# A hybrid decoder block: the gate's sigmoid from exp and log beside the attention, the transposes a step later, the residual added by an accumulating DMA

## The chip, the cores and the metric

The kernel runs on one core of a Trainium2 chip. The metric is the device time of one execution in microseconds; before the change it is 2204.19 us, the median of three runs (2201.32 to 2206.55). One execution was taken by the hardware profiler; it took 2203.55 us, and 2201.8 us of it lie between its first and its last instruction (the span). Profile lines name the engines: PE is the matrix engine (matmuls; PEld its weight loads), DVE the vector engine, ACT the scalar engine that evaluates exp, log and the like, POOL the GpSimd engine, SP the engine that only issues DMAs. Every engine executes its own list of instructions in order; an instruction that waits holds up all that stand behind it on its engine.

## The reference

One layer on 528 positions (16 learned ones ahead of 512 real ones) of width 2048, all in float32:

```python
hn = rmsnorm(h, norm_mix_g)
proj = hn @ w_in                                  # u (1024 wide), q, k, v (16 heads of 64)
y_ssm = s5_mixer(u)                               # diagonal state-space scan, GELU, then the gate:
#       y = y * sigmoid(y @ w_glu + b_glu)
y_attn = stick_breaking_attention(q, k, v)
#       z = q k^T / 8;  keep = log_sigmoid(-z) on valid keys
#       w = exp(log_sigmoid(z) + sum of keep over the later keys);  y = w v
h = h + concat(rmsnorm(y_ssm, g_ssm), rmsnorm(y_attn, g_attn)) @ w_out
hn = rmsnorm(h, norm_ffn_g)
gate, val = split(causal_depthwise_conv(hn @ w_up, 3 taps))
h = h + (silu(gate) * val) @ w_down               # 5632 wide
out = rmsnorm(h, norm_final_g)[16:]
```

## The kernel before

Everything stands transposed: channels lie on the 128 partitions, positions along the free axis. A matmul in full float32 precision is made of three fast ones (`mm3`, lines 319 to 321): each operand is split into a high part and the rest, and high times high, high times rest and rest times high are added in one PSUM bank. So each weight tile (128 by 1024) is loaded by SP, cast to its high part on ACT (`wh`, line 241), and the rest is made on DVE (`wl`, line 117 called from line 259). These splits are written two weight tiles ahead of their use.

The stages follow each other on PE: the input projection (`u` first, then k, v and q for four units of four heads each), the gate of the state-space branch (`w_glu`, eight weight tiles j, lines 1268 to 1286), the output projection in two passes (first the half that reads the state-space branch, 16 output tiles, line 1301; then the half that reads the attention, line 1385), the feed-forward up projection with a scheme of seven products, and the down projection. Between the passes and the up projection stand two places where the helper lanes are run out (`drain`).

Beside these dense stages a second stream of work runs, written as Python generators ("lanes"). While the dense matmuls are written out, `pulse` adds the nanoseconds of each group of three to a credit, and each time the credit reaches a period it takes one step of the lane. So the order of the lane's instructions among the dense ones, on every engine, is fixed when the program is written. The attention lane takes a step per `PERATT` = 900 ns of dense work. An attention unit is a preparation (k and q split, v transposed) and twelve items (a block of queries with some heads), two steps for each. An item goes through four parts that are set some steps apart by `LAGS` = (2, 4, 6):

- `stage_a`: the scores on PE, the copy out of PSUM and Abs, Exp, Ln on ACT (`at`, lines 981 to 984);
- `stage_a2`, two steps later, on DVE: max and add, a scan along the keys against a tile of ones (`steady`), and a subtraction (lines 991 to 997);
- `stage_b`, four steps after `stage_a`: PE transposes the result (line 1018; line 1008 for the last item) and ACT takes exp;
- `stage_c`, six steps after: the product with v on PE (line 1057) and the copy out on DVE (line 1064).

During the gate, and in the last input-projection tile ahead of it, `hold[0]` is set and `pulse` does nothing: the attention lane stands still. Per gate tile j there are two halves of 24 matmuls of 260 columns; after each, ACT takes the sigmoid from PSUM with the bias, and DVE multiplies with y (line 111, tile 128 x 2 x 130). After the second half ACT scales by the norm gain (line 1282), DVE makes the rest (line 1283), ACT squares, POOL adds up the squares. Sigmoid is in another function table of ACT than exp and log, so a table is loaded ahead of the gate and another behind it.

The output projection's first pass takes each output tile from PSUM with a DVE multiplication (line 1308). Then `ssm_done` loads the residual `x` through SP and POOL adds it (line 1296). `h` is used again in the second pass.

At the start nine matmuls on the tile of ones warm PE while the first inputs are on their way (line 1167).

Of the kernel before, what the change touches and what calls it, by code (L numbers as in the profile page):

```python
# [15 lines left out]
AF = mybir.ActivationFunctionType  # L16
ALU = mybir.AluOpType
# [3 lines left out]
P = 128  # L21
# [4 lines left out]
T0 = 14  # L26
LT = L - T0
# [4 lines left out]
NC4 = L // 4  # L32
NEG = -1.0e30
PERIOD = 1600.0
PERATT = 900.0

SLACK = 3
PERX = 1100.0
HOLD = True

MIR = 60
LAGS = (2, 4, 6)

V_GMIX, V_GSSM, V_GATT, V_GFFN, V_GFIN, V_BGLU, V_CB = 0, 16, 24, 32, 48, 64, 72
V_CW = V_CB + 2 * NF
# [15 lines left out]
def build(tc, io, nslots=67, manual=True):  # L61
    nc = tc.nc
    ctx = ExitStack()
    with ctx:
# [11 lines left out]
        def open_phase(name):  # L76
            if phase[0] is not None:
                phase[1].__exit__(None, None, None)
            phase[0] = None
            if name:  # L80
                phase[1] = tc.tile_pool(name=name, bufs=2)
                phase[0] = phase[1].__enter__()

        def small(shape, tag, dt=F32, bufs=1):
            uid[0] += 1
            return phase[0].tile(list(shape), dt, tag=tag, bufs=bufs, name=f"{tag}_{uid[0]}")

        V, S, G, PE = nc.vector, nc.scalar, nc.gpsimd, nc.tensor
        uid = [0]

        def slot(shape, dt=F32):
            uid[0] += 1
            return sl.tile(list(shape), dt, tag="s", name=f"s{uid[0]}")
# [3 lines left out]
        def act(out, in_, func, **kw):  # L97

            if func in (AF.Exp, AF.Ln):
                if table[0] != "explog":  # L100
                    S.preload_act_table_set("natural_log_exp_and_others")
                table[0] = "explog"
            elif func not in (AF.Abs, AF.Square, AF.Copy, AF.Identity):
                table[0] = func
            S.activation(out, in_, func, **kw)  # L105
# [4 lines left out]
        def mul(e, out, a, b):  # L110
            e.tensor_tensor(out, a, b, op=ALU.mult)  # L111

        def add(e, out, a, b):
            e.tensor_tensor(out, a, b, op=ALU.add)  # L114
# [6 lines left out]
        def vcol(off, j):  # L121
            return vec[:, off + j : off + j + 1]
# [8 lines left out]
        steady = cst.tile([P, L], F32, name="steady")  # L131
# [160 lines left out]
        lanes = []  # L292
        credit = [0.0]
        period = [PERIOD]
        hold = [False]

        def step():
            for g in list(lanes[0]):
                if next(g, "end") == "end":
                    lanes[0].remove(g)  # L300
            if not lanes[0]:
                lanes.pop(0)

        def pulse(ns):

            if hold[0]:
                return
            credit[0] += ns
            while credit[0] >= period[0]:
                credit[0] -= period[0]  # L310
                if lanes:
                    step()
# [10 lines left out]
        def bank(shape, pool=psd, tag="d"):  # L323
            uid[0] += 1
            return pool.tile(list(shape), F32, tag=tag, name=f"{tag}{uid[0]}")
# [10 lines left out]
        def dense(kts, halves, evac, mid=None, cut=lambda x, a, b: x[:, a:b]):  # L336

            n = len(kts)
            widths = [int(np.prod(cut(kts[0][0], a, b).shape[1:])) for a, b in halves]
            pss = [dbank([P, x]) for x in widths]  # L340
            for k in range(0, n, 8):
                w = next_w()
                for i, (a, b) in enumerate(halves):
                    for j in range(8):
                        xh, xl = kts[k + j]
                        mm3(pss[i], w[0][:, j, :], w[1][:, j, :], cut(xh, a, b), cut(xl, a, b), k + j == 0, k + j == n - 1)
                        if j < 7:
                            pulse(1.4 * widths[i])
                    if i == 0:
                        ahead()  # L350
                    if mid:
                        mid(k, i)
                    if k + 8 >= n:
                        evac(pss[i], a, b)
# [34 lines left out]
        def acc_square(acc, first, x, n):  # L389
            if first:  # L390
                act(acc[:, :n], x, AF.Square)
            else:
                q = slot([P, 528])
                act(q[:, :n], x, AF.Square)
                add(G, acc[:, :n], acc[:, :n], q[:, :n])
# [461 lines left out]
        QT, KTS, VT = 0, 1, 2  # L857
# [2 lines left out]
        ydone = dram.tile([8, P, LT], F32, name="ydone")  # L860

        def at_tile(n, m):
            return small([P, 528], "at", bufs=6)[:n, :m]

        class Unit:

# [60 lines left out]
            def stage_a(self, it):  # L927
# [18 lines left out]
                else:  # L946
# [32 lines left out]
                    if j == 0:  # L979
                        self.kf = self.qf = None  # L980
                t = at_tile(n, m)
                act(t, z, AF.Abs)
                act(t, t, AF.Exp, scale=-1.0)
# [95 lines left out]
        def att_lane():  # L1079
            open_phase("att")  # L1080
            period[0] = PERATT
            todo = {}
            now = [0]
            A2, B, C = LAGS

# [68 lines left out]
                add(V, accx[:, :L], accx[:, :L], q[:, :L])  # L1154
            xraw[k] = None

        G.memset(steady, 1.0)
        G.memset(epsc, EPS)

        nc.scalar.dma_start(vec, io["vec"])  # L1160
# [2 lines left out]
        act(cst.tile([P, 1], F32, name="warm"), epsc, AF.Square)  # L1163

        ps = bank([P, 264])
        for i in range(9):
            PE.matmul(ps, steady[:, :P], steady[:, :264], start=True, stop=True)
        load_x(1)
        load_x(2)
# [18 lines left out]
        for k in range(KT):  # L1188
            for j in range(3):
                i = 3 * k + j  # L1190
# [54 lines left out]
        for un in range(4):  # L1245
            for what, base in ((KTS, 16), (VT, 24), (QT, 8)):
                for p in range(2):
                    t = slot([P, L])

                    def evac(ps, a, b):  # L1250
                        if what == QT:
                            V.scalar_tensor_tensor(t[:, a:b], ps, 0.125, rstd[:, a:b], op0=ALU.mult, op1=ALU.mult)
                        else:
                            mul(V, t[:, a:b], ps, rstd[:, a:b])

                    hf = HQ if what == QT else HF
                    hold[0] = (un, what, p) == (3, QT, 1)
                    dense(xg, hf, evac, ready_y if (un, what, p) == (3, QT, 1) else None)
                    nc.sync.dma_start(qkv[what, 2 * un + p, :, hf[0][0] :], t[:, hf[0][0] :])
            qkv_ready[0] = un + 1  # L1260
# [3 lines left out]
        HG = [(0, 2), (2, 4)]  # L1264
        accs = slot([P, 528])
        y2 = []
        hold[0] = True
        for j in range(8):
            sg = slot([P, 4, NC4 - 2])
            yy = slot([P, L])  # L1270
            yr = yraw[j]
            yraw[j] = None
            y2.append((slot([P, LT], F32R), slot([P, LT], F32R)))

            def gate(ps, a, b):
                act(sg[:, a:b, :], ps.rearrange("p (t c) -> p t c", t=2), AF.Sigmoid, bias=vcol(V_BGLU, j))
                mul(V, yy[:, 8:].rearrange("p (c t) -> p t c", t=4)[:, a:b, :], yr[:, a:b, 2:], sg[:, a:b, :])

            dense(ys, HG, gate, cut=lambda x, a, b: x[:, a:b, 2:])
            for a, b in [(T0, L)] if j < 7 else [(T0, 272), (272, L)]:  # L1280
                r = slice(a - T0, b - T0)
                S.mul(y2[j][0][:, r], yy[:, a:b], vcol(V_GSSM, j))
                V.scalar_tensor_tensor(
                    y2[j][1][:, r], yy[:, a:b], vcol(V_GSSM, j), y2[j][0][:, r].bitcast(F32), op0=ALU.mult, op1=ALU.subtract
                )
            acc_square(accs, j == 0, yy[:, T0:], LT)
        hold[0] = False
        ys = yraw = None


        h = []

        def ssm_done(o, t):
            x = slot([P, LT])
            nc.sync.dma_start(x, io["xT"][o][:, T0:])
            add(G, t, t, x)
            h.append(t)


# [1 line left out]
        for o in range(KT):  # L1301
            t = slot([P, LT])

            def evac(ps, a, b):
                if o < 2:
                    S.copy(t[:, a:b], ps)
                else:
                    mul(V, t[:, a:b], ps, rs[:, a:b])

            dense(y2, HT, evac, (lambda k, i: rms(rs, accs, HT[i : i + 1], 1024, (psd, "d"))) if o == 1 else None)  # L1310
            if o == 0:
                t0 = t
            if o == 1:
                for x in (t0, t):
                    mul(V, x, x, rs[:, :LT])
                ssm_done(0, t0)
            if o:
                ssm_done(o, t)
# [66 lines left out]
        for o in ORD:  # L1385
            dense(ya, HT, lambda ps, a, b: add(V, h[o][:, a:b], h[o][:, a:b], ps))
            x = h[o]
# [140 lines left out]
        for c in range(ND):  # L1528
            for o in range(KT):
                w = next_w()  # L1530
                ps = bank([P, SEQ])
# [15 lines left out]
        for o2 in range(8):  # L1547
            w = next_w()
            for oo in range(2):
                o = 2 * o2 + oo  # L1550
                ps = bank([P, SEQ])
# [35 lines left out]
        for a, b in ((0, 256), (256, 512)):  # L1587
            for o in range(KT):
                w = ws[o // 2]
                ps = bank([P, 256])  # L1590
# [109 lines left out]
```

## Time and profile before

| what | value |
|---|---|
| median of three runs | 2204.19 us (2201.32 to 2206.55) |
| the profiled execution, its span | 2203.55 us, 2201.8 us |
| PE busy | 2155.4 us (98%) |
| DVE busy | 1570.7 us (71%) |
| ACT busy | 1052.7 us (48%) |
| POOL busy | 209.7 us (10%) |
| attention units 0 and 1, beside the k, v, q projections | about 366 to 487 us |
| the gate, attention held | 494 to 541 us |
| units 2 and 3, beside the first pass of the output projection | 541 to 672 us |
| end of the attention lane, second pass | 672 to 772 us |
| up and down projections | from 772 us to the end |

A busy PE is not a PE at its peak: matmuls are pipelined and overlap in the records, so waits shorter than about 0.15 us do not show as idle time. What is read from the profile is where PE sits idle, what it waited for, and how the other engines' instructions follow each other there.

### The profile page before, as it was taken

What the parts mean: (1) busy time and instruction counts of PE and PEld (TensorE: products, weight loads), DVE (VectorE), ACT (ScalarE), POOL (GpSimd) and SP (SyncE); (2) the same over time, 40 slices, a digit from 0 to 9 for tenths busy, and PEclk for the clock granted to TensorE, in tenths of its full rate; (3) what the DMA queues carried; (4) which work ended last, traced back from release to release, by engine and by line L of the source; (5) the groups of instructions that cost most, each with busy time, mean ns of one, the idle gap of its engine ahead of it and who ended that gap; (6) DMA issues with size and microseconds to landing.
All of it is one profiled execution on the core that took longest, in us unless ns stands there. A gap on an engine that the chain in (4) does not pass through costs nothing.

```text
span 2201.8 us, 39840 instructions
## 1 busy us (share of the span) xinstructions
PE 2155.4 (98%) x16222; PEld 2042.1 (93%) x16222; DVE 1570.7 (71%) x2363; ACT 1052.7 (48%) x1692; POOL 209.7 (10%) x290
## 2 busy tenths in 40 slices
PE   9999999999899999999999999999999999999997
PEld 9999999889789989999999999999999888888887
DVE  7977885775876778887887788778778544444454
ACT  6255444775773555455555554554555222222235
POOL 0000000001112321111111111111110000000004
PEclk9999999999999999999999999999999999999999
DMA  6433324342333367777777777777777433333342
GB/s 221 120 109 111 114 91 135 103 127 92 116 108 102 128 167 197 197 193 194 194 207 187 194 198 194 196 193 205 187 193 222 160 122 117 120 118 117 115 144 77
DMA packets 118806, 335.10 MB, mean 152 GB/s; under 512 B 13024, under 2 KB 25696, under 8 KB 118624
## 3 DMA queue, kind: packets, MB, share of 16 engines
q1 hardware_dynamic: 100144, 269.34, 38.2%
q0 software_dynamic: 17472, 61.89, 13.7%
q8 instruction: 127, 2.08, 0.4%
q10 hardware_dynamic: 1008, 1.33, 0.2%
q14 instruction: 55, 0.45, 0.1%
HBM read 300.23 MB, written 32.28 MB: 151 GB/s over the span
## 4 chain that ended last, share of the span: by engine, by line
PE 63%; DVE 2%; issue 1%; ACT 1%; DVEq 0%; ACTq 0%
PE d L320 15%; PE d L319 15%; PE d L321 15%; PE z L320 4%; PE z L319 4%; PE z L321 4%; PE y L320 2%; PE y L319 2%; PE y L321 2%; DVE s L117 0%; DVE wl L117 0%; ACT wh L241 0%; ACT s L1356 0%; DVE s L114 0%; DVE s L111 0%
## 5 line engine op out<-in xcount | busy, mean ns | idle before, releaser
L319 PE MATMUL d<-s,wh 128*128 128x258 f32 (+4 forms) x3456 | 1061.8, 307 | 6.4 <-DVE s L111 2.7
L320 PE MATMUL d<-s,wh 128*128 128x258 f32 (+4 forms) x3456 | 1054.8, 305 | 2.2 <-DVE s L117 1.2
L321 PE MATMUL d<-s,wl 128*128 128x258 f32 (+4 forms) x3456 | 1051.3, 304 | 1.2 <-DVE wl L117 1.2
L319 PEld LDWEIGHTS d<-s,wh 128*128 128x128 f32 x3456 | 653.8, 189 | 37.8 <-DVE s L114 2.7
L320 PEld LDWEIGHTS d<-s,wh 128*128 128x128 f32 x3456 | 656.6, 190 | 31.6 <-DVE s L117 2.5
L321 PEld LDWEIGHTS d<-s,wl 128*128 128x128 f32 x3456 | 658.2, 190 | 29.9 <-DVE wl L117 1.8
L241 ACT CAST wh<-wr 128x1024 fp32r<-128x1024 f32 (+2 forms) x209 | 197.5, 945 | 426.3 <-PE d L320 340.5
L114 DVE TENSOR_TENSOR s<-s,d 128x512 f32<-128x512 f32 (+2 forms) x176 | 103.7, 590 | 262.8 <-PE d L321 260.3
L117 DVE TENSOR_TENSOR wl<-wr,wh 128x1024 fp32r<-128x1024 f32 (+2 forms) x209 | 232.6, 1113 | 80.0 <-ACT wh L241 79.9
L320 PE MATMUL z<-s,wh 128*128 128x258 f32 (+1 forms) x768 | 218.4, 284 | 0.0
L319 PE MATMUL z<-s,wh 128*128 128x258 f32 (+1 forms) x768 | 217.7, 283 | 0.5 <-ACT s L1431 0.5
L321 PE MATMUL z<-s,wl 128*128 128x258 f32 (+1 forms) x768 | 217.3, 283 | 0.5 <-DVE wl L117 0.5
L117 DVE TENSOR_TENSOR wl<-wu,wh 128x1024 fp32r<-128x1024 f32 x132 | 161.5, 1224 | 2.7 <-ACT wh L241 2.7
L114 POOL TENSOR_TENSOR s<-s,s 128x514 f32<-128x514 f32 (+1 forms) x73 | 85.3, 1169 | 776.0 <-ACT s L105 663.8
L319 PE MATMUL y<-s,wh 128*128 128x258 f32 (+1 forms) x544 | 155.3, 285 | 0.0
L320 PE MATMUL y<-s,wh 128*128 128x258 f32 (+1 forms) x544 | 154.8, 285 | 0.0
L321 PE MATMUL y<-s,wl 128*128 128x258 f32 (+1 forms) x544 | 153.4, 282 | 1.2 <-DVE wl L117 1.2
L241 ACT CAST wh<-wu 128x1024 fp32r<-128x1024 f32 x132 | 138.9, 1052 | 31.8 <-ACT s L105 31.7
L321 PEld LDWEIGHTS z<-s,wl 128*128 128x128 f32 x768 | 146.4, 191 | 0.7 <-DVE wl L117 0.7
L320 PEld LDWEIGHTS z<-s,wh 128*128 128x128 f32 x768 | 145.9, 190 | 0.0
L319 PEld LDWEIGHTS z<-s,wh 128*128 128x128 f32 x768 | 144.8, 188 | 0.7 <-ACT s L1431 0.7
L117 DVE TENSOR_TENSOR wl<-wu_s,wh 128x1024 fp32r<-128x1024 f32 x88 | 107.6, 1223 | 41.2 <-ACT wh L241 41.2
(225 smaller groups left out, 2798.0 us busy)
## 6 DMA issues: line engine op xcount, KB each, us to landing
wu<-w_up SPq DMA_DIRECT2D x132, 512.0 KB, 5.2
wu_s<-w_up SPq DMA_DIRECT2D x88, 512.0 KB, 4.9
wu_s<-w_up POOLq DMA_DIRECT2D x88, 512.0 KB, 7.4
wr<-w_down SPq DMA_DIRECT2D x96, 384.0 KB, 3.0
wr<-w_in SPq DMA_DIRECT2D x63, 512.0 KB, 4.3
wr<-w_out SPq DMA_DIRECT2D x32, 512.0 KB, 3.8
fact<-s POOLq DMA_DIRECT2D x44, 256.0 KB, 2.9
s<-fact SPq DMA_DIRECT2D x44, 256.0 KB, 3.4
```

Source lines behind the costliest of these rows:

```text
L114: e.tensor_tensor(out, a, b, op=ALU.add)
L117: e.tensor_tensor(out, a, b, op=ALU.subtract)
L241: S.copy(hi[:, r], raw[:, r])
L319: PE.matmul(ps, whi, xhi, start=start, stop=False, **kw)
L320: PE.matmul(ps, whi, xlo, start=False, stop=False, **kw)
L321: PE.matmul(ps, wlo, xhi, start=False, stop=stop, **kw)
```

## The change

Six edits. (1) In the gate, DVE takes the bias and a lower bound of -87 from PSUM, and ACT makes the sigmoid as exp(-ln(1 + exp(-z))) in three instructions in place, all in the table that the attention uses; the number of table loads on ACT falls from seven to five. (2) `hold` is gone: the attention lane also steps during the gate and the tile ahead of it. (3) `PERATT` goes from 900 to 1080. (4) `LAGS` goes from (2, 4, 6) to (2, 5, 7), with seven instead of six buffers for `at`. (5) The residual is added by a DMA that accumulates into the tile, issued by POOL. (6) The tile of ones is set in two pieces, and six matmuls instead of nine warm PE.

```diff
-PERATT = 900.0
+PERATT = 1080.0
-LAGS = (2, 4, 6)
+LAGS = (2, 5, 7)
...
-        hold = [False]
...
         def pulse(ns):
-            if hold[0]:
-                return
             credit[0] += ns
...
-            return small([P, 528], "at", bufs=6)[:n, :m]
+            return small([P, 528], "at", bufs=7)[:n, :m]
...
-        G.memset(steady, 1.0)
+        G.memset(steady[:, :264], 1.0)
+        G.memset(steady[:, 264:], 1.0)
...
-        for i in range(9):
+        for i in range(6):
             PE.matmul(ps, steady[:, :P], steady[:, :264], start=True, stop=True)
...
-                    hold[0] = (un, what, p) == (3, QT, 1)
...
-        hold[0] = True
         for j in range(8):
...
             def gate(ps, a, b):
-                act(sg[:, a:b, :], ps.rearrange("p (t c) -> p t c", t=2), AF.Sigmoid, bias=vcol(V_BGLU, j))
-                mul(V, yy[:, 8:].rearrange("p (c t) -> p t c", t=4)[:, a:b, :], yr[:, a:b, 2:], sg[:, a:b, :])
+                z = sg[:, a:b, :]
+                V.tensor_scalar(z, ps.rearrange("p (t c) -> p t c", t=2), vcol(V_BGLU, j), -87.0, op0=ALU.add, op1=ALU.max)
+                act(z, z, AF.Exp, scale=-1.0)
+                act(z, z, AF.Ln, bias=1.0)
+                act(z, z, AF.Exp, scale=-1.0)
+                mul(V, yy[:, 8:].rearrange("p (c t) -> p t c", t=4)[:, a:b, :], yr[:, a:b, 2:], z)
...
-        hold[0] = False
...
         def ssm_done(o, t):
-            x = slot([P, LT])
-            nc.sync.dma_start(x, io["xT"][o][:, T0:])
-            add(G, t, t, x)
+            nc.gpsimd.dma_start(t, io["xT"][o][:, T0:], accum_op=ALU.add)
             h.append(t)
```

How the instructions stand now, at three places. The line numbers of the changed kernel are lower by two or three than before.

ACT in the gate, before: the sigmoids of two halves, the scaling, the square, and the cast of a later weight tile (`wh`), from one step j into the next.

```order
L105 ACTIVATE s924_6528<-d928_6532,vec_77 128x260
L105 ACTIVATE s924_6528<-d929_6533,vec_77 128x260
L1282 ACTIVATE s926_6530<-s925_6529,vec_77 128x514
L105 ACTIVATE s930_6594<-s925_6529 128x514
L241 CAST wh69_6627<-wr69_6493 128x1024
L105 ACTIVATE s931_6597<-d935_6601,vec_77 128x260
```

ACT in the gate, now, step j = 3 (the gate's tile is s981): `at` and 128x384 or 128x512 rows are the attention's.

```order
L241 CAST wh69_6888<-wr69_6602 128x1024
L105 ACTIVATE s981_6824<-s981_6824 128x260 x3
L105 ACTIVATE s997_6912<-z996_6908 128x384
L105 ACTIVATE at_1004_6935<-s993_6869 128x384
L105 ACTIVATE at_1004_6935<-at_1004_6935 128x384 x2
L105 ACTIVATE s1007_6956<-z1006_6952 128x384
L105 ACTIVATE s981_6824<-s981_6824 128x260 x3
L1283 ACTIVATE s983_6826<-s982_6825,vec_77 128x514
L105 ACTIVATE s1008_6968<-s982_6825 128x514
L974 COPY s1017_6996<-z1015_6986 128x512
L974 COPY s1018_6998<-z1016_6987 128x512
L105 ACTIVATE at_1019_7000<-s1017_6996 128x512
```

Behind these rows follow Exp and Ln of the same `at`, one exp of 128x384, and the next cast. What was one instruction per half is three in place on the gate's tile, with an item of the attention between the halves.

DVE in the gate, before: the rest of a weight tile, the two multiplications, the rest of the scaled tile.

```order
L117 TENSOR_TENSOR wl70_6698<-wr70_6562,wh70_6696 128x1024
L111 TENSOR_TENSOR s939_6667<-s890_6270,s938_6666 128x2x130 x2
L1283 SCALAR_TENSOR_TENSOR s941_6669<-s939_6667,vec_77,s940_6668 128x514
L117 TENSOR_TENSOR wl71_6767<-wr71_6631,wh71_6765 128x1024
L111 TENSOR_TENSOR s946_6736<-s891_6272,s945_6735 128x2x130 x2
```

DVE in the gate, now, the same step j = 3.

```order
L117 TENSOR_TENSOR wl69_6890<-wr69_6602,wh69_6888 128x1024
L1274 TENSOR_SCALAR s981_6824<-d985_6828,vec_77 128x260
L111 TENSOR_TENSOR s982_6825<-s860_6147,s981_6824 128x2x130
L1061 COPY s941_6543<-y987_6836 128x128
L1061 COPY s942_6544<-y987_6836 128x128
L988 SCALAR_TENSOR_TENSOR at_994_6871<-s992_6867,at_994_6871 128x384
L991 SCALAR_TENSOR_TENSOR at_1005_6939<-steady_83,at_994_6871 128x384
L117 TENSOR_TENSOR at_1005_6939<-s992_6867,at_1005_6939 128x384
L1274 TENSOR_SCALAR s981_6824<-d986_6829,vec_77 128x260
L111 TENSOR_TENSOR s982_6825<-s860_6147,s981_6824 128x2x130
L1284 SCALAR_TENSOR_TENSOR s984_6827<-s982_6825,vec_77,s983_6826 128x514
L988 SCALAR_TENSOR_TENSOR at_1004_6935<-s993_6869,at_1004_6935 128x384
```

The new instruction on PSUM stands behind `wl` of a weight tile and directly ahead of the multiplication that reads its result through ACT; an attention item (lines 988 to 994, three instructions) stands between the halves.

PE at the first transposes (line 1018, now 1015) of unit 0, before: they stand directly behind the scores of the item two later.

```order
L967 MATMUL z682_4983<-s650_4805,s658_4843 128x256
L967 MATMUL z681_4982<-s649_4804,s659_4844 128x256
L967 MATMUL z682_4983<-s649_4804,s659_4844 128x256
L1018 MATMUL z685_4999<-consts_78,at_680_4960 128x116 x4
L319 MATMUL d656_4832<-s57_349,wh53_4778 128x264
L320 MATMUL d656_4832<-s58_350,wh53_4778 128x264
```

And now: twelve dense matmuls stand between those scores and the transposes, and nine behind them ahead of the next scores.

```order
L318 MATMUL d653_4819<-s55_331,wl53_4778 128x264
L316 MATMUL d687_5042<-s14_133,wh54_4868 128x264
L317 MATMUL d687_5042<-s15_134,wh54_4868 128x264
L318 MATMUL d687_5042<-s14_133,wl54_4870 128x264
L1015 MATMUL z689_5047<-consts_78,at_680_4973 128x116 x4
L316 MATMUL d687_5042<-s16_143,wh54_4868 128x264
L317 MATMUL d687_5042<-s17_144,wh54_4868 128x264
```

Over the whole program the attention of units 2 and 3 moves forward: unit 2 now begins in the last tile ahead of the gate and fills most of the gate, unit 3 begins late in the gate, and the lane ends about five of the sixteen output tiles of the first pass earlier than before.

## The prediction

> **What bounds the kernel now.** First the page: the span, the engines, and the chain that ended last.
>
> ```profile
> span 2201.8 us, 39840 instructions
> PE 2155.4 (98%) x16222; PEld 2042.1 (93%) x16222; DVE 1570.7 (71%) x2363; ACT 1052.7 (48%) x1692; POOL 209.7 (10%) x290
> PE 63%; DVE 2%; issue 1%; ACT 1%; DVEq 0%; ACTq 0%
> ```
>
> PE is the bound, and the change leaves its matmuls as they are but for three warm-up ones. So the time can only move by what PE waits. The second view is the list of PE's waits in the stretches that the change touches: units 0 and 1 (366 to 478 us), units 2 and 3 (541 to 672), the end of the lane (672 to 730). Columns: total us, times, longest.
>
> ```profile
> PE z L1018 <- DVE at L117: 5.7, 8, 1.3
> ...
> PE z L1018 <- DVE at L117: 8.6, 7, 2.0
> PE z L1018 <- ACT s L977: 2.1, 1, 2.1
> PE z L1008 <- DVE at L117: 1.7, 1, 1.7
> ...
> PE d L319 <- DVE s L111: 2.7, 2, 2.0
> ```
>
> The transposes wait for DVE's last attention part: 5.7 us in units 0 and 1, 12.4 in units 2 and 3, and 2.7 at the lane's end. That is 20.8 us, and the most that a longer lag can win, but for refilling PE after each wait. Third, the stretch view: PE, PEld, DVE, ACT and POOL busy, clock, DMA. The gate alone, and the first matmul of each three (line 319) while units 2 and 3 run:
>
> ```profile
> 494.00:541.00 47.00, 47.00 (x367) 46.88 (x367) 26.56 (x32) 23.70 (x38) 7.88 (x6) 0.94 0.29 96
> 541.00:672.00 131.00, 55.13 (x180) 34.93 (x179) 0.97 0.33 106
> ```
>
> The gate is PE from end to end: 384 matmuls in 47 us, 0.122 us each. From 541 to 672 us 3 x 180 dense matmuls take 66 us by that price; less 12.4 of waits, 52.6 us are left for two units, 26 us of PE for one.
>
> **The transposes a step later, the slower lane.** A transposition may now come five steps behind its scores and DVE's part two behind, so DVE has three steps instead of two, each 1080 instead of 900 ns of dense work: 3.2 instead of 1.8 us. The added 1.4 us covers all waits quoted but the longest of 2.0 and 2.1. The residual's 16 POOL additions stood in the same stretch as units 2 and 3, and DVE is slower beside them. DVE with the tile of 384 columns, first while POOL adds (571.25 to 574.48 us), then alone:
>
> ```profile
> 571.25 3.23 POOL L114 TENSOR_TENSOR s<-s,s 128x514 f32<-128x514 f32 x2 [12.10 <-DVE s L111]
> ...
> 571.69 1.65 DVE L991 SCALAR_TENSOR_TENSOR at<-s,at 128x384 f32<-128x384 f32 x1
> 573.37 1.93 DVE L994 TENSOR_TENSOR_SCAN at<-steady,at 128x384 f32<-128x384 f32 x1
> ...
> 577.28 0.48 DVE L1064 COPY s<-y 128x128 f32<-128x128 f32 x2
> 577.67 0.55 DVE L991 SCALAR_TENSOR_TENSOR at<-s,at 128x384 f32<-128x384 f32 x1
> 578.26 0.96 DVE L994 TENSOR_TENSOR_SCAN at<-steady,at 128x384 f32<-128x384 f32 x1
> 579.25 0.56 DVE L117 TENSOR_TENSOR at<-s,at 128x384 f32<-128x384 f32 x1
> ```
>
> 1.65 and 1.93 against 0.55 and 0.96: about 1 us per instruction met. With both gone I take 20 of the 20.8 us (ends 10, if only the longer lag at the old DVE speed counted, and 25 with the refills).
>
> **Attention in the gate.** This decides. What must follow what there is in the order rows quoted with the change. The prices are those of the gate before:
>
> ```profile
> 507.17 0.73 ACT L1282 ACTIVATE s<-s,vec 128x514 fp32r<-128x514 f32 x1 [0.69 <-DVE s L111]
> 507.80 0.62 ACT L105 ACTIVATE s<-s 128x514 f32<-128x514 f32 x1
> 508.33 1.03 ACT L241 CAST wh<-wr 128x1024 fp32r<-128x1024 f32 x1
> 509.26 0.47 ACT L105 ACTIVATE s<-d,vec 128x260 f32<-128x260 f32 x1
> ...
> 503.55 1.23 DVE L117 TENSOR_TENSOR wl<-wr,wh 128x1024 fp32r<-128x1024 f32 x1 [0.71 <-ACT wh L241]
> 504.69 0.62 DVE L111 TENSOR_TENSOR s<-s,s 128x260 f32<-128x260 f32 x1
> 506.51 0.62 DVE L111 TENSOR_TENSOR s<-s,s 128x260 f32<-128x260 f32 x1 [1.20 <-ACT s L105]
> ```
>
> and those of the attention on ACT (copies, Abs, Exp and Ln, exp), with the two forms nearest to the new ones: exp of 258 columns on ACT, and a DVE operation with a scalar on 258 columns of PSUM.
>
> ```profile
> 576.59 0.49 ACT L105 ACTIVATE s<-z 128x384 f32<-128x384 f32 x1 [0.77 <-PE z L1018]
> 576.98 0.51 ACT L105 ACTIVATE at<-s 128x384 f32<-128x384 f32 x1
> ...
> 590.68 1.07 ACT L977 COPY s<-z 128x512 f32<-128x512 f32 x2 [0.52 <-PE z L967]
> 591.64 0.64 ACT L105 ACTIVATE at<-s 128x512 f32<-128x512 f32 x1
> 592.31 1.30 ACT L105 ACTIVATE at<-at 128x512 f32<-128x512 f32 x2
> 593.51 0.58 ACT L105 ACTIVATE s<-z 128x512 f32<-128x512 f32 x1
> ...
> L105 ACT ACTIVATE s<-s 128x258 f32<-128x258 f32 x2 | 0.8, 415 | 0.0
> ...
> L371 DVE TENSOR_SCALAR s<-y 128x258 f32<-128x258 f32 x1 | 0.4, 427 | 2.1 <-ACT s L105 2.1
> ```
>
> An instruction that reads what the last one wrote starts about 0.03 us after its end (Abs 0.64, Exp 0.67 later); an independent one starts some 0.1 before that end.
>
> Now one step of the gate, j = 3, from cast to cast, along what each waits for. The cast of the weight tile, 1.03 and 0.04 until DVE takes it: 1.07. On DVE the rest of the tile and then the new instruction on PSUM, 1.14 and 0.43: 1.57; ACT stands, since its next instruction reads that result. Exp, Ln, Exp, 3 x 0.445: 1.33; DVE stands, since its next multiplies by it. The multiplication (0.55 to the next start), two copies (0.39), the item's three (577.67 to 579.25 and 0.48, so 2.06), the second half's instruction on PSUM (0.43): 3.43; ACT has only exp, Abs, Exp, Ln and exp of 384 columns meanwhile, about 2.4, and stands for 1. The second Exp, Ln, Exp: 1.33. The multiplication until ACT may scale: 0.66 (506.51 to 507.17), ACT stands. Scaling 0.63, square 0.53, two copies 0.96, Abs, Exp, Ln 1.87 (591.64 to 593.51), exp 0.39: 4.38. Sum 1.07 + 1.57 + 1.33 + 3.43 + 1.33 + 0.66 + 4.38 = 13.8 us.
>
> PE needs for the same step 47/8 = 5.9 us of dense work and a sixth of a unit: from the last tile ahead of the gate to the first pass the lane goes through one unit and a third, 1.33 x 26 = 34 us in eight steps, 4.3 each. 10.2 against 13.8. PE cannot run ahead for long: the product with v waits for an exp that ACT makes two steps of the lane earlier. The other steps hold other rows (four scans for 116 rows; two items of 512 columns; the splits of unit 3) and come to 13.9 to 16.6 in the same walk; I take 14.5 on average. From the first half's end: 6.5 for the rest of step 0, 7 x 14.5 = 101.5, and 1 until the output projection has the last tile, 109 us. PE's own work there: 47 - 2.9 for the first half, 34, and 3.6 until it needs that tile, 81.7. PE waits 27 us. The lower end is ACT's own work, without its standing: 13.8 - 1.57 - 1 - 0.66 = 10.6 per step, 0.4 over PE, 3 us in eight; the upper end is 16 per step, 38 us.
>
> The table load ahead of the gate and that behind it were 1.28 us each on ACT, beside PE's work:
>
> ```profile
> 494.70 1.28 ACT L105 ACT_TABLE_LOAD   x1
> 496.00 0.48 ACT L105 ACTIVATE s<-d,vec 128x260 f32<-128x260 f32 x1
> ```
>
> They give nothing back while ACT stands 3.2 us per step anyway. The Trainium skill ("ScalarE: Activation LUTs", section "What ACT_TABLE_LOAD costs") puts a switch at 2.66 us, load and drain; by it ACT would be spared 5.3 instead of 2.6 us. In the trace the sigmoid starts 0.02 us behind the load's end, so no drain shows, and the sum is the same by both.
>
> The casts of y ahead of the gate wait for a DMA, PE 1.2 us with them:
>
> ```profile
> PE d L320 <- DVE s L117: 1.2, 4, 0.4
> ```
>
> Unit 1's end and unit 2's preparation now stand in the same queues behind those casts: +2 (0 to 5).
>
> **The rest.** The 16 accumulating DMAs go through POOL's queue, where the additions were. The nearest row is POOL's 16 stores of h, 0.57 us each; 0.57 replaces an addition of 1.3, and SP loses 16 loads. They are wanted a whole pass (over 90 us) later. Nothing, either way. Fewer warm-ups: PE could start about 1 us earlier, but its next wait, for DVE's split of x at 12.6 us, ends when that input is there. Nothing; 1 us at most.
>
> ```profile
> PE d L320 <- DVE s L415: 0.9, 1, 0.9
> L1331 POOL DMA_DIRECT2D hres<-s x16 | 9.1, 568 | 58.1 <-DVE s L114 58.1
> ```
>
> **Sum.** The profiled execution took 2203.55, 0.6 below the median of the runs. -20 + 27 + 2 = +9, so 2212.6 by the profile and 2213 against the median. The 0.2% that a measurement of this kernel tells from no change are 4.4 us: 2199.8 to 2208.6.
>
> **The rivals.** (a) Faster: the gate does not stand on the alternation of ACT and DVE but on ACT's own work, so that the steps take 10.6 us. For it speaks that the sum 13.8 hangs on short rows that I took in strict order; against it that both engines' order is written out, and each link is a read of what the one before wrote. Then -20 + 3 + 2: 2189. It decides where a step takes under 12.6 us, since 8 x 2.4 = 19 then cancels the 20 won. (b) No difference: steps of 12.6 us, or 13.8 and somewhat more won outside: 2204. (c) Slower still, by the clock. In the starvation ahead of the gate PE was given half its clock afterwards:
>
> ```profile
> 488.00:494.00 6.00, 4.46 (x22) 3.23 (x22) 4.13 (x8) 4.06 (x7) 0.00 (x0) 0.88 0.82 231
> 494.00:500.00 6.00, 6.00 (x30) 5.88 (x30) 2.58 (x4) 2.44 (x3) 0.00 (x0) 0.55 0.60 219
> ```
>
> 30 matmuls instead of 49 in those 6 us cost 19 x 0.122 = 2.3 us. Once per step that hides in the 3.6 us that PE waits anyway; twice it sticks out by 1 us, so +8 in eight steps, and with the same in the passes around it 2225. The Trainium skill ("TensorE: Matmul & The Clock Gate", section "Why this matters for your kernels") asks for no gap over about 3 us between bursts; here waits of 0.4 us with PE busy three quarters of the time were enough, so the trace is harsher than that sentence.
>
> **How the numbers follow.** My forecast, steps of 13 to 15.5 us: 0.50. Slower still by the clock or by steps of 16: 0.16. No difference: 0.12. Faster: 0.22. Slower 0.66, same 0.12, faster 0.22. The forecast's own range is 2206 to 2221. To hold 8 in 10 the range takes in the clock's 2225 with some of the upper end, and reaches down over the no-difference case to 2192, the slower part of (a).
>
> **What would show it.** Right: in the stretch of the gate (about 494 us to some 103 to 110 us later) DVE and ACT wait for each other, PE's waits there come to 20 to 35 us, and the transposes' waits in units 0, 1 and 3 fall under 3 us. Scans beside POOL additions at 1.9 us should be left only beside the squares' sums. Wrong: PE waits under 15 us in the gate, or the transposes outside it still wait 10 us.

## The result, and the profile after

The changed kernel takes 2223.79 us (median of four runs, 2223.68 to 2224.71) against 2203.53 (2201.32 to 2206.55) for the kernel before on the same chip: a ratio of 1.0092, 95% interval 1.0074 to 1.0109, or 20.3 us more. The profiled execution took 2223.89 us. From its page, the span, PE's line and the chain that ended last by engine:

```profile
span 2222.1 us, 39849 instructions
...
PE 2165.0 (97%) x16216; PEld 2051.0 (92%) x16216; DVE 1567.3 (71%) x2379; ACT 1062.7 (48%) x1722; POOL 197.0 (9%) x291
...
PE 87%; DVE 6%; ACT 4%; issue 2%; DMA 0%; SPq 0%; DVEq 0%; ACTq 0%
```

In the chain DVE and ACT now hold 10% where they held 3%. The stretch view from the first instruction on the gate's PSUM to the last (columns as before), and PE's waits in it:

```profile
494.00:604.50 110.50, 82.16 (x669) 73.61 (x669) 71.25 (x117) 79.00 (x166) 10.77 (x13) 0.88 0.19 63
```

```profile
PE y L1054 <- ACT s L105: 10.5, 3, 8.4
PE z L1015 <- DVE at L117: 9.6, 4, 4.5
PE z L913 <- ACT s L911: 3.0, 1, 3.0
PE z L953 <- ACT s L974: 2.7, 1, 2.7
PE y L1054 <- DVE s L1061: 2.5, 1, 2.5
```

No engine is busy more than 75% of the time there, and PE's granted clock is 0.88. One step of the gate, j = 3, from cast to cast (ACT and DVE with one row of POOL, in order of time):

```profile
534.27 1.03 ACT L241 CAST wh<-wr 128x1024 fp32r<-128x1024 f32 x1
...
535.34 1.23 DVE L117 TENSOR_TENSOR wl<-wr,wh 128x1024 fp32r<-128x1024 f32 x1 [0.33 <-ACT wh L241]
...
536.48 0.48 DVE L1274 TENSOR_SCALAR s<-d,vec 128x260 f32<-128x260 f32 x1
...
537.00 1.33 ACT L105 ACTIVATE s<-s 128x260 f32<-128x260 f32 x3 [1.69 <-DVE s L1274]
...
538.36 0.64 DVE L111 TENSOR_TENSOR s<-s,s 128x260 f32<-128x260 f32 x1 [1.39 <-ACT s L105]
...
539.22 0.55 DVE L988 SCALAR_TENSOR_TENSOR at<-s,at 128x384 f32<-128x384 f32 x1
...
541.27 0.48 DVE L1274 TENSOR_SCALAR s<-d,vec 128x260 f32<-128x260 f32 x1
...
541.79 1.32 ACT L105 ACTIVATE s<-s 128x260 f32<-128x260 f32 x3 [1.19 <-DVE s L1274]
...
543.15 0.63 DVE L111 TENSOR_TENSOR s<-s,s 128x260 f32<-128x260 f32 x1 [1.39 <-ACT s L105]
...
543.81 0.72 ACT L1283 ACTIVATE s<-s,vec 128x514 fp32r<-128x514 f32 x1 [0.70 <-DVE s L111]
...
545.20 1.27 POOL L114 TENSOR_TENSOR s<-s,s 128x514 f32<-128x514 f32 x1 [12.19 <-ACT s L105]
...
545.24 1.65 DVE L988 SCALAR_TENSOR_TENSOR at<-s,at 128x384 f32<-128x384 f32 x1
...
548.15 1.04 ACT L241 CAST wh<-wr 128x1024 fp32r<-128x1024 f32 x1
```

Each bracket on ACT and DVE is one of them standing for the other: ACT 1.69, 1.19 and 0.70 us, DVE 0.33, 1.39 and 1.39. From cast to cast it is 13.88 us.

Behind the gate (606 to 740 us) PE's listed waits are down to three groups, and none of them is a transposition's:

```profile
PE d L316 <- ACT s L1283: 2.5, 1, 2.5
PE d L316 <- DVE s L111: 2.1, 2, 2.0
PE y L1054 <- ACT at L105: 0.2, 1, 0.2
```

For the ledger the traces are cut by the count of dense groups of three, so that every stretch holds the same dense work. From each interval between the starts of two matmuls the median interval of that kind of matmul (traces of before and changed kernel; 0.122 us in the gate) is taken off. What remains is lost time: waits, and matmuls at the slow clock. In us, of the profiled executions:

| kernel | units 0, 1 (840 to 1024) | gate (1024 to 1152) | output projection, first pass (to 1408) | second pass (to 1560) | time, median |
|---|---|---|---|---|---|
| before | 11.3 | 6.0 | 27.1 | 1.3 | 2203.5 |
| changed | 6.5 | 46.4 | 11.5 | 1.0 | 2223.8 |

In the other three columns 20.7 us are won and in the gate 40.4 lost; that is 19.7 of the 20.3 us. The lane's own matmuls at their medians are 44.3 us in units 2 and 3 before; in the changed kernel 25.5 of them stand in the gate.

### The profile page after: what moved, and what is told of

Its sections match the earlier page's. It is cut to its first block, busy times and chain, and to the rows that moved or that the text cites. A ratio compares the mean times of both kernels' runs of the same rounds, so it can differ in the third digit from the quotient of the medians.

```text
span 2222.1 us, 39849 instructions
## 1 busy us (share of the span) xinstructions
PE 2165.0 (97%) x16216; PEld 2051.0 (92%) x16216; DVE 1567.3 (71%) x2379; ACT 1062.7 (48%) x1722; POOL 197.0 (9%) x291
## 4 chain that ended last, share of the span: by engine, by line
PE 87%; DVE 6%; ACT 4%; issue 2%; DMA 0%; SPq 0%; DVEq 0%; ACTq 0%
PE d L316 21%; PE d L317 21%; PE d L318 20%; PE z L317 4%; PE z L316 4%; PE z L318 4%; PE y L317 3%; PE y L316 3%; PE y L318 3%; ACT s L105 2%; DVE s L111 1%; DVE wl L117 1%; DVE s L117 1%; ACT at L105 1%; DVE at L991 1%
## 5 line engine op out<-in xcount | busy, mean ns | idle before, releaser
L105 ACT ACTIVATE s<-s 128x260 f32<-128x260 f32 (+8 forms) x230 | 113.4, 501 | 65.0 <-DVE s L1274 26.9
```

## The experiments

The comparisons are with the kernel before on the same chip; its median lay between 2202.4 and 2203.7, so a difference of 1 us between two experiments is not to be read.

**PE's work in the gate.** In the gate `mm2`, two matmuls, stands for `mm3`; this kernel leaves out the product of the weights' rest, and its output is that much less exact.

```diff
-    mm3(pss[i], w[0][:, j, :], w[1][:, j, :], ...)
+    (mm2 if two else mm3)(pss[i], w[0][:, j, :], w[1][:, j, :], ...)
```

> The changed kernel with a third of the gate's dense matmuls left out (the product of the weights' low part; its output is that much less exact): 128 matmuls of 260 columns, 15.6 us of PE work less at full clock. Theory A (the gate's length is set by ACT and DVE waiting for each other): the time stays within 4 us of the changed kernel's 2224, PE only waits 12 to 16 us more. Rival C (PE's half clock behind each wait lengthens the gate): 8 to 16 us less, 2208 to 2216, or more if the half clock counts twice.

Measured: 2224.98, ratio 1.0096 (1.0081 to 1.0111). The same stretch of it:

```profile
494.00:604.50 110.50, 74.89 (x561) 64.39 (x561) 71.66 (x117) 79.24 (x167) 11.76 (x13) 0.79 0.18 63
```

In this stretch there are 108 matmuls fewer (128 in the whole gate), ACT and DVE are as busy as before, PE's listed waits grow from 28.3 to 36.8 us, the clock is lower still (0.79) and the time is unchanged. PE and its clock do not set the length of the gate; theory A holds, rival C falls.

**No DVE instruction between PE and ACT.** `nb` is the negated bias, made once. The lower bound of -87 goes with the instruction.

```diff
-    V.tensor_scalar(z, ps..., vcol(V_BGLU, j), -87.0, op0=ALU.add, op1=ALU.max)
-    act(z, z, AF.Exp, scale=-1.0)
+    act(z, ps..., AF.Exp, bias=nb[:, j : j + 1], scale=-1.0)
```

> The changed kernel without DVE's instruction between PE and ACT in the gate: the first exp reads PSUM itself, with a negated bias (made once); the clamp at -87 falls away. ACT no longer waits for DVE's split of the weights and that instruction (1.07 + 1.57 on the chain become one cast of 1.03), nor for it at the second half (0.43). Theory A (alternation): a step falls from 13.8 to about 11.1 us, 8 x 2.7 = 21 us less, about 2203 (2198 to 2210). Rival C (the clock, or PE's own waits for the attention, set the gate's length): 0 to 8 us less, 2216 to 2224.

Measured: 2200.06, ratio 0.9983 (0.9974 to 0.9992), 23.7 us under the changed kernel. The gate's lost time falls from 46.4 to 22.5 us, 3.0 per step where 2.7 were expected. Among ACT's waits from 494 to 577 us the 26.7 us for the instruction on PSUM are gone (the changed kernel's line stands with the next experiment); the longest that is left is the multiplication:

```profile
ACT s L1284 <- DVE s L111: 5.7, 7, 1.5
```

Some 16 us of the gate's 40 stay without the crossing. They come with the attention beside the gate: held and without the crossing, the gate loses 6.6 us (period 900, below), about what it lost before. Which of the attention's instructions make them was not taken apart.

**Orders alone.** In one run the multiplications and the tile's scaling come half a tile or a tile later; in another the first half's sigmoid goes ahead of the next weight tile's cast and split.

```diff
-    mul(V, yy[...], yr[...], z)
+    for f in late: f()
+    late.clear()
+    late.append(lambda: mul(V, yy[...], yr[...], z))   # and the scaling, rest and square behind it
```

```diff
-    if i == 0: ahead()
     if k + 8 >= n: evac(pss[i], a, b)
+    if i == 0: ahead()          # in the gate only
```

> The changed kernel with the gate's second end later: each half's multiplication by the sigmoid is issued on DVE behind the next half's first instruction and its three of ACT, and a tile's scaling, rest and square behind the next tile's first half. DVE then does not stand for the three of ACT (1.33, twice a step), and ACT not for the multiplication (0.66); what stays is ACT's own 10.6 us of a step and its wait of 1.57 for the split and the instruction on PSUM. Theory A: a step falls from 13.8 to about 12.2, 13 us less, about 2211 (2206 to 2216). Rival C (the clock, or PE's own waits): no change, 2220 to 2228.

> The changed kernel with one order changed: in the gate the first half's sigmoid is issued ahead of the next weight tile's cast and split instead of behind them, on ACT and DVE both. Nothing is added or left out. Theory A: the first instruction on PSUM no longer stands behind the split, so ACT is spared 1.07 + 1.14 of its wait less what the cast then has to wait; 1.1 to 1.6 us per step, 9 to 13 in all, 2211 to 2215. Rival I (the split then comes late, PE waits for the weights instead): 2220 to 2230.

Measured: 2222.81 (ratio 1.0086, 1.0069 to 1.0103) and 2224.65 (1.0092, 1.0075 to 1.0109): neither gains, my expectations of 13 and 9 to 13 us were wrong, and both times lie in the ranges of the rivals. The causes that these named are not borne out: the time did not follow PE's work above, and with the other order no wait of PE for the weights is listed in the gate. ACT's waits for the instruction on PSUM from 494 to 604.5 us, in the changed kernel, with the later multiplications, and with the other order:

```profile
ACT s L105 <- DVE s L1274: 26.7, 15, 4.3
```

```profile
ACT s L105 <- DVE s L1275: 28.7, 14, 4.2
```

```profile
ACT s L105 <- DVE s L1276: 22.1, 14, 4.1
```

With the later multiplications DVE does not stand for the sigmoid any more (20.9 us of waits before), yet ACT stands as long as it did for the instruction on PSUM. With the other order ACT waits 1.08 instead of 1.69 at the first half of j = 3, and 1.84 instead of 1.19 at the second, because the split of the weight tile now stands ahead of the second on DVE, beside the item's three instructions. The 4.6 us that its line has less do not shorten the gate: seven steps take 15.04 us on average, against 15.15. Of what was tried here only removing the crossing helped.

**Held or not, with or without the crossing.** First the changed kernel with `hold` put back, then the same with the period 900, then that without the DVE instruction, and last the period 900 without that instruction and without `hold`.

```diff
+    hold[0] = (un, what, p) == (3, QT, 1)     # and True during the gate
```

> The changed kernel with one part undone: attention is held again during the gate's last tile ahead and the eight gate steps; the sigmoid from exp and log, the longer lags, the accumulating DMA stay. Theory A (the whole loss is PE starving in the gate while the attention runs there: 46 us of waits and half-clock there against 6 before): the gate is about 47 us long again and the 20 us that the transposes gave elsewhere stay won, so 2224 - 40 = about 2184; up to 10 more if units 2 and 3, which at a step of 1080 instead of 900 ns need about a fifth more passes, are not through when the output projection ends (2184 to 2194). Rival B (part of the loss lies outside of the gate, or the transposes' saving came only from having less attention beside the output projection): 2200 or more.

Measured: 2220.66, 1.0073 (1.0058 to 1.0088). Theory A missed by 30 us and rival B's range holds. Two things cost there. The lane, at 1080 ns a step, does not end within the first pass of the output projection (28.6 us lost there, 7.0 behind it), and the held gate still loses 14.4 us.

> The run with held attention and the sigmoid from exp and log, with the lane's period set back from 1080 to 900. There the gate took 61.4 us (52.8 before) and the lane, not through when the output projection ended, cost some 20 us in waits and uncovered attention at its end. Theory A: the lane's end is covered again, the gate stays 61, so 2183 + 9 = about 2192 (2189 to 2197). Rival F (attention at this density behind the gate waits as much with the longer lags): 2203 or more.

Measured: 2214.03, 1.0047 (1.0030 to 1.0064). Theory A missed here too. The gate takes 65.5 us where I expected 61 (18.8 us lost), a wait of 8.5 follows it, and the first pass of the output projection loses 28.5 with that wait: rival F's range holds. PE's waits from 495 to 562 us, and a step with no attention in it:

```profile
PE d L319 <- DVE s L1279: 8.6, 5, 2.4
PE y L1057 <- ACT s L105: 8.5, 1, 8.5
```

```profile
523.75 1.03 ACT L241 CAST wh<-wr 128x1024 fp32r<-128x1024 f32 x1
...
524.81 1.53 DVE L117 TENSOR_TENSOR wl<-wr,wh 128x1024 fp32r<-128x1024 f32 x1 [0.70 <-ACT wh L241]
...
526.26 0.47 DVE L1279 TENSOR_SCALAR s<-d,vec 128x260 f32<-128x260 f32 x1
...
526.77 1.33 ACT L105 ACTIVATE s<-s 128x260 f32<-128x260 f32 x3 [1.99 <-DVE s L1279]
...
528.13 0.63 DVE L111 TENSOR_TENSOR s<-s,s 128x260 f32<-128x260 f32 x1 [1.39 <-ACT s L105]
...
529.10 1.32 ACT L105 ACTIVATE s<-s 128x260 f32<-128x260 f32 x3 [1.00 <-DVE s L1279]
```

Even alone the alternation takes 8.5 us a step, longer than PE's 5.9 us of dense work: PE waits for DVE to free the PSUM bank, and attention's first exp behind the gate stands behind the last chain.

> Held attention, period 900, longer lags, accumulating DMA, and the sigmoid from exp and log, but its first exp reads PSUM itself (negated bias, no clamp): against the run with held attention and period 900 only DVE's instruction between PE and ACT is gone. There the gate took 65.5 us instead of 52.8, and PE then waited 8.5 us for the exp queued behind the gate's last chain. Theory A (ACT's wait for DVE's split and that instruction makes both): the gate is 53 us again and the wait behind it about 3, so 2214 - 13 - 6 = about 2195, as with the table's sigmoid. Rival G (three ACT instructions instead of one make the gate longer, whoever feeds them): 2205 to 2214.

Measured: 2195.21, 0.9959 (0.9944 to 0.9974), as expected. The same place of its step: the exp follows the cast at once, and no bracket shows a wait for DVE.

```profile
522.12 1.04 ACT L241 CAST wh<-wr 128x1024 fp32r<-128x1024 f32 x1
523.06 0.47 ACT L105 ACTIVATE s<-d,nb 128x260 f32<-128x260 f32 x1
523.55 0.88 ACT L105 ACTIVATE s<-s 128x260 f32<-128x260 f32 x2
524.74 0.48 ACT L105 ACTIVATE s<-d,nb 128x260 f32<-128x260 f32 x1 [0.31 <-PE d L321]
```

> The run without DVE's instruction in the gate (2200, attention not held) with the period 900 instead of 1080, so a fifth more attention beside the gate and less behind it. Theory A: that gate's step is ACT's own work (76 of 87 us busy); a fifth more attention adds 1.1 us to each of eight steps, +9, and takes a few us of waits from the passes behind: 2203 to 2209. Rival H (PE's total is the bound once the instruction is gone, and attention is better early): 2192 to 2199.

Measured: 2217.91, 1.0060 (1.0045 to 1.0075), worse than both ranges. The gate lost 38.9 us against 22.5 at 1080. In the 184 dense groups ahead of the gate the lane had taken 533 instead of 425 matmuls, so other items met the gate; which of them made the difference was not separated.

**Lags, DMA and pace.** In the kernel before, with its table sigmoid and held attention, the other edits one by one.

```diff
-LAGS = (2, 4, 6)
+LAGS = (2, 5, 7)             # and bufs=7
```

> The kernel before with the longer lags alone: LAGS (2, 5, 7) and a seventh buffer for them; period 900, held attention, sigmoid and POOL's additions as before. Theory A (the lags cover DVE's part, whatever shares the chip with it): PE's waits and half clock between 373 and 488 us and from 541 to 704 us fall from 38 us together to about 20, so 2203 - 18 = about 2185 (2182 to 2191). Rival D (the saving in the changed kernel came from the slower lane, 1080 instead of 900 ns per step, and from having less attention beside the output projection): 2198 to 2204.

Measured: 2198.63, 0.9977 (0.9968 to 0.9986), only 5 us, in rival D's range. From 541 to 740 us the transposes' waits for DVE fall from 10.3 to 4.1 us, but the product with v now waits, for DVE's copies and ACT's exp:

```profile
PE y L1057 <- DVE s L1064: 5.0, 2, 3.5
PE z L1018 <- DVE at L117: 3.3, 2, 1.8
PE y L1057 <- ACT s L105: 2.8, 1, 2.8
```

> The kernel before with the accumulating DMA alone in place of the loads and POOL's 16 additions. Theory A: DVE's scans in units 2 and 3 no longer meet POOL's additions; where a transposition waited for a slowed scan 1 to 2 us go, so -2 to -6, 2197 to 2201. Rival E (the slowed scans did not set the waits): within 2 us of 2203.

Measured (edit: the `ssm_done` of the change): 2196.59, 0.9969 (0.9957 to 0.9980), 7 us, a little more than expected. The lost time in the first pass of the output projection falls from 27.1 to 19.6.

> The kernel before with the longer lags (and the seventh buffer) and the accumulating DMA; period 900, held attention and the table's sigmoid as before. Theory A (the two parts outside of the gate won 20 us in the changed kernel and do so without the gate's part): 2203 - 20 = about 2183 (2180 to 2188), the fastest of all. Rival D (they need the slower lane): 2196 to 2204.

Measured: 2195.03, 0.9964 (0.9951 to 0.9977). The two do not add up to 12: 8.6 us, short of the 20 of theory A.

The next four differ in the period, and start as the changed kernel does (six warm-ups, the memory set in two parts).

> The run with the longer lags and the accumulating DMA alone (2195), with the period 975 instead of 900 and the changed kernel's start (six warm-ups, the memory set in two parts). The lane would end about triple 1376 of 1408 instead of 1346. Theory: DVE's part has 3 x 975 ns, and the product with v waits less for DVE's copies; -1 to -4 and -0.5 from the start, 2190 to 2194. Rival (the waits left are handovers at the units' ends, whatever the pace): 2194 to 2196; if the lane is not through by the end of the output projection: over 2200.

Measured: 2185.93, 0.9916 (0.9902 to 0.9931), better than expected and the fastest version of all, 17 us under the kernel before and 38 under the changed one. The matmuls do not wait for the casts of y any more, and the transposes wait 0.7 us for DVE's part and once 2.6 for ACT. What is left from 524 to 740 us begins with the lane's end:

```profile
PE d L320 <- DVE s L404: 3.8, 4, 1.9
PE z L1018 <- ACT at L105: 2.6, 1, 2.6
PE y L1057 <- DVE s L1064: 1.7, 2, 1.3
PE z L1008 <- DVE at L117: 0.7, 1, 0.7
```

> The fastest run without the longer lags: LAGS (2, 4, 6) and six buffers as before; accumulating DMA, period 975, short start. Rival D (the slower lane, not the lag, takes the waits away): 2184 to 2189. Theory A (the lag does it: DVE's two steps grow from 1.8 to 1.95 us only, so most transposes still wait): 2191 to 2197, the accumulating DMA's 7 us and a few more.

Measured: 2200.67, 0.9992 (0.9983 to 1.0002), above both expected ranges; the transposes still wait 7.1 us for DVE's part. Without the longer lags the slower pace costs 4 us (2196.6 at 900); with them it wins 9.

> The fastest run with the period 940 instead of 975. The lane's end, which cost 7 us between the output projection and the up projection at 975 (8.3 of waits and slow clock there, 1.3 before), is covered again; the waits inside of units 2 and 3 (12.3 at 975, 21.2 at 900) come to some 16. -7 + 4: about 2183 (2180 to 2187). Rival N (a unit's handovers fall on other instructions at every pace, with no trend): 2187 to 2195.

Measured: 2192.59, 0.9953 (0.9938 to 0.9967). The lane's end is covered again (1.4 us lost there instead of 8.3), but the first pass loses 19.9 instead of 12.3. My sum missed; in so far as there is no smooth trend between 900, 940 and 975, rival N holds.

> The fastest run with the period 1080, the changed kernel's, and attention held as before. Theory L (at this pace with held attention the lane isn't through when the output projection ends, and its last part runs with no dense matmuls beside it): the run with held attention and 1080 took 2221, of which the instruction between PE and ACT made 19 (2214 against 2195 at 900), so about 2202 (2198 to 2206). Rival M (the longer pace removes more waits than the end costs): under 2186.

Measured: 2200.85, 0.9991 (0.9981 to 1.0000), theory L. Its two longest waits from 521 to 760 us are the lane's last part with no dense work beside it:

```profile
PE d L319 <- ACT s L400: 6.7, 1, 6.7
PE y L367 <- POOL s L114: 4.5, 1, 4.5
```

> The changed kernel with the period 975 instead of 1080, so that it differs from the fastest run (2186: longer lags, accumulating DMA, 975, short start) only in the gate's sigmoid and in not holding the attention there. Theory J (the gate's part costs about 37 us at whatever pace, and more with more attention in it; with the sigmoid read from PSUM 900 took 18 us more than 1080): 2224 to 2240. Rival K (much of the changed kernel's loss is its pace of 1080): 2205 to 2215.

Measured: 2225.87, 1.0102 (1.0087 to 1.0118), theory J. At an equal pace of 975 the gate's part costs 2225.9 - 2185.9 = 40 us, what the ledger says for the changed kernel.

The lost time and the medians of these runs, for the table above:

| run | units 0, 1 | gate | first pass | second pass | time |
|---|---|---|---|---|---|
| exp and log from PSUM, not held, 1080 | 6.4 | 22.5 | 10.7 | 1.0 | 2200.1 |
| exp and log by DVE, held, 900 | 7.0 | 18.8 | 28.5 | 1.2 | 2214.0 |
| exp and log from PSUM, held, 900 | 6.9 | 6.6 | 22.7 | 1.3 | 2195.2 |
| lags and DMA, 900 | 6.9 | 6.1 | 21.2 | 1.2 | 2195.0 |
| lags and DMA, 975 | 6.5 | -0.2 | 12.3 | 8.3 | 2185.9 |
| lags and DMA, 1080 | 5.9 | 1.4 | 22.8 | 7.5 | 2200.9 |

## Why the prediction was right and wrong

The sign, the place and the alternation of ACT and DVE were right, the size was not: +9 by the sum, +20.3 measured, above the forecast's own range (2206 to 2221) though inside of the whole one.

Its own signs of being right came true: ACT and DVE stand for each other, PE's listed waits in the gate are 28.3 us, and no transposition waits in units 0 and 1 or behind the gate. They could not show the miss, since the listed waits are not all the time that PE loses.

**The transposes (-20).** 20.7 us were won outside of the gate, nearly what the sum had, but in part by luck. Of its 20.8 us, 4.8 were no waits of transposes for DVE's part: 2.1 waited for ACT's copy (L977), and 2.7 were dense matmuls that waited for a DVE multiplication (L111), of which 2.1 remain. The wait of 1.7 was also longer than the 1.4 us that the lag adds. And only part of what was won is the lag's. With all the attention of units 2 and 3 still behind the gate, lags and DMA gave 8.6 us at 900, since the product with v then waits for DVE's copies and ACT's exp, and 17 at 975. In the changed kernel 25.5 of 44.3 us of attention had moved into the gate, where its waits count as the gate's; there the transposes wait 9.6 us for DVE's part again.

**The gate (+27 and the casts of y, +2; measured 40).** The mechanism held, and so did the walk: 13.88 us for j = 3 against 13.8, and 28.3 us of listed waits against 27. Both sides of the difference were off, though. PE's first matmul of the gate's second half starts at 487.50, its first on the last tile at 608.13: 120.6 us, where I had 109 for the stretch and 81.7 for PE's own work.

The first failing step is that own work: "52.6 us are left for two units, 26 us of PE for one", and one unit and a third. I had taken off only the 12.4 us of listed waits. By the ledger some 24 us are lost there (27.1 up to the end of the first pass); the rest, short waits and the slow clock, I counted as work. At their medians the lane's matmuls take 44.3 / 2 = 22 us for one unit, and 26.2 of them stand in the stretch, 1.2 units. With 46.5 of dense matmuls PE's own work is 72.7, 9 less than assumed.

The second is the start. The first instruction on PSUM stands at 493.35, 5.9 us after PE had gone on, because DVE had not a gap in its queue until then: the splits of y, unit 1's last item, unit 2's preparation (from the timeline of DVE).

```profile
487.35 1.32 DVE L117 TENSOR_TENSOR s<-s,s 128x528 fp32r<-128x528 f32 x2
488.58 0.69 DVE L988 SCALAR_TENSOR_TENSOR at<-s,at 64x528 f32<-64x528 f32 x1
489.31 1.25 DVE L991 TENSOR_TENSOR_SCAN at<-steady,at 64x528 f32<-64x528 f32 x1
...
493.35 0.48 DVE L1274 TENSOR_SCALAR s<-d,vec 128x260 f32<-128x260 f32 x1
```

I had put +2 (0 to 5) on these casts and what stands behind them. Start and end of the stretch took 14.6 us, not 7.5. The third is the mean of the other steps: seven took 15.15 us (493.35 to 599.40), not 14.5; the longest took 17.1, and unit 3's preparation stands in the last two (15.6 and 16.7). Together 120.6 - 72.7 = 48 us are lost in that stretch, 2.5 of it in the wait for the last tile that the ledger counts to the next column, and 6 were lost in the gate before.

**The DMA (0):** alone it is worth 7 us; the sum had POOL's part of this inside of the transposes' 20. **Table loads (0):** right; held, the sigmoid from exp and log out of PSUM takes 2195.2 and the table's sigmoid with its two loads 2195.0. **Warm-ups:** the first dense matmul starts 0.85 us earlier, and 0.2 of it is left after 30 us.

**The rivals.** (a) would have needed steps of 12.6 us; seven came to 15.15 on average. Without the crossing seven steps take 12.2 us on average, and the time is 2200, not its 2189. (c) named nearly the right time, 2225, but not for its reason: half clock there is (0.88, 0.79 with fewer matmuls), and the time does not depend on it; that it came so near was luck. (b), no difference, would have needed the same steps or more won outside, and neither came. Lags, DMA and a period of 1080 with held attention give about its time (2200.9), but for another reason: there the lane's end eats the saving.

## What to carry to other kernels

Two engines that work in order and hand one tile back and forth cost by the crossing, not by the instruction: one 0.48-us instruction on DVE between PE and ACT cost 19 us in eight steps with the attention held and 24 with it beside the gate. Reordering around it gained nothing, and letting ACT read PSUM with its own bias (without the lower bound) took that cost away. To set a wait against an engine's work, add up that work from its instructions at full clock; a stretch less its listed waits still holds the short waits and the slow clock. A lag between stages and the pace of the lane belong together: the slower pace alone lost 4 us and with the longer lag won 9, and the lane still has to end under the cover of dense work.

## What the runs showed of the hardware

A DVE instruction with two operands in SBUF stood until POOL's was through. In the step above POOL's addition runs from 545.20 to 546.47, and DVE's, started at 545.24, ends at 546.89, 0.42 after it, where it takes 0.55 alone. The Trainium skill ("SBUF — State Buffer", section "SBUF: two separate sides") calls the ports that the two share an exclusive lock, held for the whole instruction; these rows agree with it. With POOL's 16 additions gone the kernel before ran 7 us faster; how much of that is this contention was not separated.

PE's clock fell after waits that were short beside its work. In the held gate with DVE's instruction no wait is over 2.4 us (8.6 in five) and PE is busy 44 of 53 us, yet the clock granted is 0.94 on average. Behind two of the waits of 2.4 us it is 0.5 for 3.4 us each, and the matmuls of 260 columns start every 0.21 us instead of 0.12. Without the instruction it is 1.00 over nearly the same matmuls (the two stretches, with and without it):

```profile
495.00:548.00 53.00, 44.44 (x331) 43.40 (x331) 25.91 (x38) 29.54 (x57) 6.47 (x5) 0.94 0.18 62
```

```profile
495.00:536.00 41.00, 41.00 (x338) 41.00 (x337) 23.14 (x27) 32.93 (x63) 7.92 (x6) 1.00 0.24 80
```
